# A transformer layer step on one core: small products moved to column quarters of TensorE, state products regrouped, and the loads and waits around them rearranged

## The chip, the cores and the metric

The kernel runs on one core of one Trainium2 chip, as one program. The metric is the device time of one execution in microseconds (us), inputs and outputs in device memory; smaller is better.

## What is computed

The reference is one step of a hybrid decoder layer for two groups of requests at once: a prompt of 256 tokens and 8 samples of 8 tokens each (past length 2048, paged cache). Model width is 1024, all in float32:

```python
x = x + 0.5 * swiglu_ffn(rmsnorm(x, ffn1_norm), ffn1_w_in, ffn1_w_out)      # 1024 -> 2 x 2816 -> 1024
h = rmsnorm(x, mix_norm)
z, xbc, dt_raw, q, kv, nsa_g, merge_g = jnp.split(h @ w_in_proj, cuts, axis=-1)
y_ssm, new_conv, new_ssm = mamba_mixer(...)        # conv, SSD with state (8, 32 heads, 64, 128) for the samples
q = rmsnorm(q.reshape(...), qk_norm[0]) * (HEAD_DIM ** -0.5)                # 16 heads of 64
o, new_win = nsa_fn(...)       # three branches: compressed blocks of 32 rows, top-16 blocks of 64, window of 512
mix = (gm[..., :D_MODEL] * (y_ssm @ w_branch_ssm) + gm[..., D_MODEL:] * (o @ w_branch_attn)) @ w_out
x = x + mix
x = x + 0.5 * swiglu_ffn(rmsnorm(x, ffn2_norm), ffn2_w_in, ffn2_w_out)
```

The compressed keys and values are `silu((rows + pe) @ w1) @ w2` over blocks of 32 rows, of the prompt and of the whole cache; relative biases come from a table of 32 buckets.

## The kernel before

All activations are kept transposed, features on the 128 partitions and the 320 tokens (256 of the prompt, 64 of the samples) along the free axis. A product with a big weight is a call of `dense` (L332). The weights come in 245 blocks of 128x1024 numbers, one after the other, through `w_load` (L300) on SyncE's DMA queue into buffers named `wraw`. ScalarE casts a block to its high part `wh` (`w_hi`, L314), VectorE subtracts that to get the low part `wl` (`w_lo`, L323); both are fp32r, the matmul form in which one pass suffices. TensorE then does three products for each of the 8 slices of 128 rows: high weight by high activation (L342), high by low (L343), low by high (L344), 24 products a block, each with 320 columns. Other products are in plain fp32 and appear in the trace as two instructions each.

The order of everything is set by the Python program. `dense` is its backbone: FFN1, then the projections (q and k, v, xBC, merge gates, z), the two branch products, the output product, FFN2. All other work is written as generators that `Sched.tick` steps between the slices of `dense`, by a credit that grows with `RATE`; `yield from wait(n)` lets n steps pass, and `S.defer(n, f)` calls f after 2n ticks, that is n quarters of a block. Each engine executes its own instructions strictly in the order so written, and the DMA queues of SyncE (SP) and GpSimd (POOL) do too.

The small work that the change touches, in order of time:

- During FFN1 the generator `cmp_stream` compresses the cache. It first turns the bias table into `trev` with products against a one-hot matrix `oh` (L638). `positions` (L599) sums 16 products of a slice of `w1` (128x128, stationary) with one column of position embedding (L602), once for keys and once for values. `cmp_keys` ends that work with two groups of four products (L733).
- `prompt_bias` (L840) loads the prompt's bias rows and a 128x128 `flip` matrix (L849) into `blob`, loads `tb` and `cb`, bias rows for the samples (`load_bias`, L832, 8 DMAs each), and multiplies by `flip` (L855).
- For each of the 12 blocks of q and k, the squares are summed over each head by one fp32 product with 24 output rows (L1870). `qk_norm` takes roots on 24 partitions and spreads them to the 128 feature rows by an fp32 product with a contraction over 24 rows (L873), again once per block.
- `prompt_cmp` compresses the prompt's rows: 16 fp32 products of a slice of `w1` with 32 columns (L1053), twice.
- `ssd` (chunks with the products L1637 and L1658, POOL multiplications L1627) and `sample_chunks` (state update of the samples) run during the xBC, merge and z projections. There are 32 states of 128x512 (`h`, 4 quarters q times 8 samples b), loaded by `load_h` (L1726) four ahead into 6 buffers, stored by `store` (L1679). Two at a time they are multiplied with `cz` on two column quarters of 32 (L1772); each is scaled on POOL (L1775), and a product `bz` x (`xh`, `xl`) is added: L1778 with 128 contraction rows, L1779 with 64, both fp32r with 512 columns; VectorE adds the result to `h` (L1780).
- `Squares` (L355) collects squares for a norm: `acc` on POOL or VectorE, then 12 instructions with one output column (L392: 3 token groups, `acc` and the last square apart).
- The sample attention loads pages `KV` (L1384) and multiplies them in eight tiles at once (L1431). `early_bias` (L1386) loads its bias rows, 16 DMAs on SP's queue (L1393).

Of the kernel before, what the change touches and what calls it, by code (L numbers as in the profile page):

```python
# [22 lines left out]
NB = 8  # L23
T = 8
# [19 lines left out]
_C = {}  # L44
_off = 0
for _n, _w in (("id", 128), ("sq", 47), ("sg", 7), ("tm", 8), ("gsum", 32), ("ex", 128), ("ss", 128), ("trp", 128),
               ("trs", 64), ("rm", 8), ("flip", 128), ("gs", 384), ("gp", 48)):
    _C[_n] = (_off, _w)
    _off += _w
# [8 lines left out]
def constants():  # L58
# [8 lines left out]
    a = np.zeros((128, 47)); a[p, 22 + p // 64] = 1; put("sq", a)  # L67
# [48 lines left out]
RATE = (0.59, 1.2, 0.9, 1.5, 0.85, 1.0, 1.0)  # L116
# [5 lines left out]
class Sched:  # L122
# [8 lines left out]
    def defer(self, n, f):  # L131
        self.later.append([n, f])
# [62 lines left out]
def step_kernel(ctx, tc, I, O):  # L195
# [102 lines left out]
    NRAW, SA = 2, 2  # L298
# [33 lines left out]
    def dense(unit, xh, xl, out, cut=1, extra=None):  # L332

        k0, K = 0, sum(n for _, n in unit)
        for i, n in unit:
# [3 lines left out]
            for k in range(n):  # L339
# [7 lines left out]
                if k == 1:  # L347
                    w_lo()
# [5 lines left out]
    class Squares:  # L354


        def __init__(self, n, delay=0):
            self.n, self.i, self.delay = n, 0, delay
# [28 lines left out]
        def sums(self):  # L387
            self.col = bank("pt", (128, 3))
            for i in range(3):
                n = 128 if i < 2 else 64  # L390
                for s in (self.acc, self.last):
                    pe.matmul(self.col[:n, i : i + 1], s[:, 128 * i : 128 * i + n], ones[:, 0:1], start=s is self.acc,  # L392
                              stop=s is self.last)
# [118 lines left out]
    for i in range(4):  # L512
        sp.dma_start(x[:, 2 * i : 2 * i + 2, :], I["xT"][:, 2 * i : 2 * i + 2, :])
        if i == 1:
            w_load()
# [5 lines left out]
    kraw = kT.rearrange("p b (a d) -> p b a d", a=2)  # L521
    kss = cp.tile([128, NB, 2], F32, name="kss")
    krs = cp.tile([128, NB, 2], F32, name="krs")
    pew = cp.tile([128, 2], F32, name="pew")
    rel = fp.tile([NBK + 1, 32], F32, name="rel")
# [72 lines left out]
    def positions(c):  # L598
        p = bank("po", (128, 1))  # L599
        for j in range(16):  # L600
            o = P_PE + 16 * c + j
            pe.matmul(p, w1raw(c)[:, j, :], par[:, o : o + 1], start=j == 0, stop=j == 15)  # L602
        v.tensor_copy(pew[:, c : c + 1], p)
        release(("w", c))

    def cmp_stream():
# [14 lines left out]
        yield  # L621
        g.memset(rel, -BIG)
# [3 lines left out]
        oht = fp.tile([NBK + 1, TL - 2048], F32, tag="hid", bufs=1, name="oht")  # L626
        sp.dma_start(oh, I["oh"][:, 0:2048])
        sp.dma_start(oht, I["oh"][:, 2048:])
# [6 lines left out]
        for k in (0, 320, 640, 960, 1280, 1600, 1920, 2048):  # L635
            n = min(NT, 2048 - k) if k < 2048 else TL - k
            p = bank("sc", (32, NT))
            pe.matmul(p[:, :n], rel, oh[:, k : k + n] if k < 2048 else oht, start=True, stop=True)  # L638
# [3 lines left out]
            yield  # L642
        release("oh")
        for q in range(4):
# [3 lines left out]
        positions(0)  # L648
        split_hi(0, 0)
        load(2)  # L650
        yield
        split_lo(0, 0)
# [3 lines left out]
        for s in range(NS):  # L656
            c, b = divmod(s, NB)
            ph = bank("sc", (128, 256))
            for q in range(4):
# [23 lines left out]
                if s == NB - 1:  # L683
                    split_w1(1, q)
                    if q == 3:
                        positions(1)
# [31 lines left out]
    def cmp_keys():  # L718
# [10 lines left out]
        yield from wait(4)  # L729
# [82 lines left out]
    cmpP = w1t[:, 4096:5120].rearrange("p (c a b i) -> p c a b i", c=2, a=2, b=2)  # L812
    q0 = ExitStack()
    pq = q0.enter_context(tc.tile_pool(name="pq", bufs=1))
    tb = pq.tile([128, 8], F32, name="tb")
# [1343 lines left out]
```

## Time and profile before

| what | value |
|---|---|
| median of 3 runs | 1389.86 us (1389.57 to 1399.72) |
| the profiled execution, its own time | 1398.44 us |
| its span in the trace | 1396.4 us |
| mean granted TensorE clock | 0.961 |
| busy: PE, DVE, ACT, POOL | 1329.4, 866.0, 592.8, 363.5 us |
| moved by DMA | 251.66 MB, 180 GB/s over the span |

A profile page shows one execution. "PE" is TensorE's matmuls, "PEld" its weight loads, DVE is VectorE, ACT ScalarE, POOL GpSimd, SP SyncE. A row such as `L342 PE MATMUL ps_pd<-hh,wh 128*128 128x320 f32 x1320 | 452.5, 343 | 4.5 ...` reads: line, engine, operation, output and inputs by the program's names, the tile of the array in use (contraction rows by output columns), the moving operand, how many, then busy time, mean ns of one, and the idle time just before them with what ended it. Matmuls overlap: the durations are longer than the distance from start to start, so what one costs is read from the starts in the timeline. PEclk is the share of the full clock that TensorE was granted.

### The profile page before, as it was taken

The page shows a single profiled execution, that of the slowest core. Times are in us where ns is not written, and L with a number is a line of the kernel's source. Part 1 is how long each engine was busy: PE and PEld are TensorE (multiplying, and loading weights), DVE is VectorE, ACT ScalarE, POOL GpSimd, SP SyncE. Part 2 cuts the span into 40 slices and gives each one's busy share as a digit, 9 for nine tenths or more (in the row PEclk, how much of TensorE's full clock was granted, in tenths as well). Part 3 has the DMA queues.
Part 4 walks back from the last instruction along what each step waited for, and adds up shares of the span by engine and source line. Part 5 has one row for each costly group of instructions (what it writes and reads, how often), then busy time and mean ns, then how long its engine had stood idle before and what let it go on. Part 6 is the DMA issues. An engine that isn't in the chain of part 4 may idle for free.

```text
span 1396.4 us, 28186 instructions
## 1 busy us (share of the span) xinstructions
PE 1329.4 (95%) x10583; PEld 1177.7 (84%) x10583; DVE 866.0 (62%) x1862; ACT 592.8 (42%) x1152; POOL 363.5 (26%) x616
## 2 busy tenths in 40 slices
PE   8999999999979999889989989799999999999998
PEld 7899999999858878677877756577677999999998
DVE  5577656655556457866567657657767766666533
ACT  4454543445434324446544343255555344333322
POOL 2222212222000216554444435233340010000000
PEclk9999999999989999889999999999999999999999
DMA  7556656666544325421177686778894443444453
GB/s 258 164 192 201 221 184 198 210 205 201 209 100 126 125 96 198 182 91 61 50 197 214 190 237 181 290 249 314 267 333 148 168 140 134 149 149 151 148 171 110
DMA packets 107041, 251.66 MB, mean 180 GB/s; under 512 B 23208, under 2 KB 49849, under 8 KB 104953
## 3 DMA queue, kind: packets, MB, share of 16 engines
q1 hardware_dynamic: 89946, 198.27, 44.2%
q0 software_dynamic: 16960, 51.61, 11.1%
q8 instruction: 83, 1.36, 0.4%
q14 instruction: 52, 0.43, 0.1%
HBM read 235.11 MB, written 23.10 MB: 185 GB/s over the span
## 4 chain that ended last, share of the span: by engine, by line
PE 72%; DVE 11%; DMA 5%; issue 4%; ACT 4%; SPq 2%; POOL 1%; POOLq 0%; ACTq 0%; DVEq 0%
PE ps_pd L342 18%; PE ps_pd L343 16%; PE ps_pd L344 16%; DVE wl L323 3%; PE ps_sc L671 2%; PE ps_sc L672 2%; PE ps_sc L681 2%; ACT wh L314 2%; PE ps_sc L1431 2%; DVE cvo L1198 2%; PE ps_po L1471 1%; DMA out_ssmS<-h 1%; PE ps_pt L1457 1%; PE ps_po L1319 1%; PE ps_sc L1270 1%
## 5 line engine op out<-in xcount | busy, mean ns | idle before, releaser
L323 DVE TENSOR_TENSOR wl<-wraw,wh 128x1024 fp32r<-128x1024 f32 (+1 forms) x245 | 302.0, 1233 | 266.9 <-ACT wh L314 266.4
L342 PE MATMUL ps_pd<-hh,wh 128*128 128x320 f32 x1320 | 452.5, 343 | 4.5 <-ACT hh L751 1.8
L343 PE MATMUL ps_pd<-hl,wh 128*128 128x320 f32 x1320 | 418.0, 317 | 1.6 <-DVE hl L450 1.4
L344 PE MATMUL ps_pd<-hh,wl 128*128 128x320 f32 x1320 | 417.2, 316 | 0.0
L314 ACT CAST wh<-wraw 128x1024 fp32r<-128x1024 f32 (+1 forms) x245 | 252.7, 1031 | 167.2 <-PE ps_pd L343 125.0
L342 PEld LDWEIGHTS ps_pd<-hh,wh 128*128 128x128 f32 x1320 | 257.4, 195 | 44.6 <-issue 32.8
L343 PEld LDWEIGHTS ps_pd<-hl,wh 128*128 128x128 f32 x1320 | 257.6, 195 | 10.2 <-issue 5.3
L344 PEld LDWEIGHTS ps_pd<-hh,wl 128*128 128x128 f32 x1320 | 256.5, 194 | 0.0
L342 PE MATMUL ps_pd<-ah,wh 128*128 128x320 f32 x352 | 109.4, 311 | 0.0
L344 PE MATMUL ps_pd<-ah,wl 128*128 128x320 f32 x352 | 108.7, 309 | 0.0
L343 PE MATMUL ps_pd<-al,wh 128*128 128x320 f32 x320 | 98.7, 309 | 0.0
L563 POOL DMA_DIRECT2D pg<-in_cache x136 | 74.3, 547 | 73.6 <-DVE pgl L575 30.6
L235 POOL TENSOR_SCALAR ah<-ff 128x320 fp32r<-128x320 f32 x44 | 20.1, 458 | 277.9 <-DVE ff L478 277.8
L575 DVE TENSOR_TENSOR pgl<-pg,pgh 128x512 fp32r<-128x512 f32 x128 | 82.4, 685 | 15.1 <-ACT pgh L568 14.9
L1384 POOL DMA_DIRECT2D KV<-in_cache x102 | 55.0, 539 | 104.3 <-PE ps_po L1471 68.5
L473 ACT ACTIVATE sg<-sg 128x320 f32<-128x320 f32 x44 | 20.8, 472 | 135.1 <-DVE sg L472 135.0
L568 ACT CAST pgh<-pg 128x512 fp32r<-128x512 f32 x128 | 72.6, 616 | 9.0 <-PE ps_sc L672 7.3
L671 PE MATMUL ps_sc<-pgh,w1h 128*128 128x256 f32 x256 | 68.6, 289 | 2.5 <-ACT pgh L568 2.5
L672 PE MATMUL ps_sc<-pgh,w1l 128*128 128x256 f32 x256 | 68.6, 288 | 0.0
L342 PEld LDWEIGHTS ps_pd<-ah,wh 128*128 128x128 f32 x352 | 66.1, 188 | 0.5
L344 PEld LDWEIGHTS ps_pd<-ah,wl 128*128 128x128 f32 x352 | 66.1, 188 | 0.0
L343 PEld LDWEIGHTS ps_pd<-al,wh 128*128 128x128 f32 x320 | 60.2, 188 | 0.0
(453 smaller groups left out, 2250.2 us busy)
## 6 DMA issues: line engine op xcount, KB each, us to landing
wraw<-in_wproj SPq DMA_DIRECT2D x77, 512.0 KB
KV<-in_cache POOLq DMA_DIRECT2D x102, 256.0 KB, 5.4
wraw<-in_w1in SPq DMA_DIRECT2D x44, 512.0 KB
wraw<-in_w2in SPq DMA_DIRECT2D x44, 512.0 KB
pg<-in_cache POOLq DMA_DIRECT2D x136, 128.0 KB, 4.1
pg<-in_cache SPq DMA_DIRECT2D x120, 128.0 KB
wraw<-in_w1out SPq DMA_DIRECT2D x16, 512.0 KB
h<-in_ssm SPq DMA_DIRECT2D x32, 256.0 KB
```

The costliest lines, as they stand in the source:

```text
L314: a.copy(h[:, :n], st["raw"][i][:, :n])
L323: v.tensor_tensor(l[:, :n], st["raw"].pop(i)[:, :n], st["hl"][i][0][:, :n], op=ALU.subtract)
L342: pe.matmul(out, wh[:, s], xh[:, kk, :], start=kk == 0, stop=False)
L343: pe.matmul(out, wh[:, s], xl[:, kk, :], start=False, stop=False)
L344: pe.matmul(out, wl[:, s], xh[:, kk, :], start=False, stop=kk == K - 1)
L563: e.dma_start(page(s, half)[:, i, :], I["cache"][ds(r, 1), :, 256 * c : 256 * c + 256].rearrange("o p f -> p (o f)"))
L568: a.copy(h[:, 8 * half : 8 * half + 8, :], page(s, half)[:, :, 64 * q : 64 * q + 64])
L575: v.tensor_tensor(l[:, 8 * half : 8 * half + 8, :], page(s, half)[:, :, 64 * q : 64 * q + 64], h[:, 8 * half : 8 * half + 8, :], op=ALU.su ...
L671: pe.matmul(ph, wh[:, j, :], h[:, :, j, :], start=q + j == 0, stop=False)
L672: pe.matmul(ph, wl[:, j, :], h[:, :, j, :], start=False, stop=False)
L681: pe.matmul(ph, wh[:, j, :], l[:, :, j, :], start=False, stop=q + j == 6)
L1384: e.dma_start(t[:, j, :], I["cache"][ds(r, 1), :, 512:1024].rearrange("o p f -> p (o f)"))
```

## The change

Line numbers with "after" are those of the changed kernel.

1. Column quarters: squares of four blocks of q and k at a time go to four quarters of 32 output columns (L1907 after, 3 groups). `positions` (L608 after) and the prompt's compression (L1083 after) swap their operands: a 32-column slice is stationary, `w1` moves, four quarters in turn, and a join product with `four32` (L615 and L1089 after) adds the quarters up.
2. Roots: taken on all 128 partitions, split into `qrh` and `qrl`, and spread with two fp32r products over 128 rows (L903 after) in place of one fp32 product over 24 rows.
3. `tb` and `cb` are no longer loaded from `trev`; 24 small products in FFN1 (L667 after, 8, 63 and 1 columns) compute them. `flip` is loaded during FFN1, `prompt_bias` is started ahead of the loads of `w1c`.
4. State update: four states at a time on four quarters (L1810 after), `xl` has 128 rows like `xh` (L1815 and L1816 after), `load_h` comes ahead of the store, five ahead into 8 buffers.
5. `Squares` may fold the last square into `acc` on VectorE, which leaves one product where there were two (z groups and the final norm).
6. Waits and rates: `cmp_keys` 4 to 7, six more steps before the first sample chunk, `WS` 8 to 4, `NRAW` 2 to 3, `w_lo` one slice later, `RATE[4]` 0.85 to 0.88, the descriptor space for software DMAs 8192 to 4096, `defer` keeps its list sorted.

The diff, cut to what the prediction speaks of:

```diff
-W0, W1, W2, W3, WS, EB = 3, 3, 6, 1, 8, 2
+W0, W1, W2, W3, WS, EB = 3, 3, 6, 1, 4, 2
...
-    NRAW, SA = 2, 2
+    NRAW, SA = 3, 2
...
-                if k == 1:
+                if k == 2:
                     w_lo()
...
         def gather(self, e):
-            if 1 < self.i < self.n:
+            if 1 < self.i < self.n + self.fold:
                 e.tensor_tensor(self.acc, self.acc, self.last, op=ALU.add)
 
         def add(self, x):
             self.square(x)
-            self.gather(g)
+            self.gather(v if self.i == self.n else g)
...
-                for s in (self.acc, self.last):
+                parts = [self.acc] if self.fold else [self.acc, self.last]
+                for s in parts:
...
     def positions(c):
-        p = bank("po", (128, 1))
+
+        p = bank("po", (128, 128))
         for j in range(16):
-            o = P_PE + 16 * c + j
-            pe.matmul(p, w1raw(c)[:, j, :], par[:, o : o + 1], start=j == 0, stop=j == 15)
-        v.tensor_copy(pew[:, c : c + 1], p)
+            o, r = P_PE + 16 * c + j, 32 * (j % 4)
+            pe.matmul(p[r : r + 32, :], par[:, o : o + 32], w1raw(c)[:, j, :], start=j < 4, stop=j >= 12)
+        pz = tp.tile([128, NT], F32, tag="sq", name="pz")[:, 0:128]
+        v.tensor_copy(pz, p)
         release(("w", c))
+
+        def join():
+            p = bank("po", (128, 1))
+            pe.matmul(p, pz, four32[:, 0:1], start=True, stop=True)
+            v.tensor_copy(pew[:, c : c + 1], p)
+
+        return join
...
+        p = bank("sc", (128, 72))
+        last = lambda t: oht[:, 6 - t : 7 - t] if t < 7 else oh[:, 2047:2048]
+        for o, n, src in ((0, 8, lambda t: oht[:, 7 - t : 15 - t]), (8, 63, lambda t: oh[:, 38 - t : 2048 - t : 32][:, 0:63]),
+                          (71, 1, last)):
+            for t in range(T):
+                pe.matmul(p[:, o : o + n], relz[:, 7 - t : 135 - t], src(t), start=t == 0, stop=t == T - 1)
+        a.copy(kcv[:, 2048:2120], p)
         release("oh")
+        sp.dma_start(flip, I["con"][:, C_KEEP : C_KEEP + 128])
...
-        yield from wait(4)
+        yield from wait(7)
...
-        flip = st["blob"][:, 4600:4728]
-        sp.dma_start(flip, I["con"][:, C_KEEP : C_KEEP + 128])
-        load_bias(tb, PAST, 8)
-        load_bias(cb, 31, 64, 32)
         yield from wait(8)
...
-            pe.matmul(bc, st["sel"][:, 128 * i : 128 * i + 128], rs, start=True, stop=True)
+            for x_ in range(2):
+                pe.matmul(bc, st["sel"][:, i, :], rhl[x_], start=x_ == 0, stop=x_ == 1)
...
+            part = bank("sc", (128, 128))
+            for j in range(16):
+                r = 32 * (j % 4)
+                pe.matmul(part[r : r + 32, :], cmpP[:, c, j].rearrange("p a b n -> p (a b n)"), w1b[:, c, j, :],
+                          start=j < 4, stop=j >= 12)
+            pz = st["blob"][:, 2688:2816]
+            v.tensor_copy(pz, part)
+            yield from wait(2)
             ph = bank("sc", (128, 32))
-            for j in range(16):
-                rhs = cmpP[:, c].rearrange("p a b (n j) -> p (a b) n j", j=16)[:, :, :, j]
-                pe.matmul(ph, w1b[:, c, j, :], rhs, start=j == 0, stop=j == 15)
+            pe.matmul(ph, pz, four32, start=True, stop=True)
...
-        NH, AHEAD = 6, 4
+        NH, AHEAD = 8, 5
...
-            xl = sx.tile([64, 512], F32R, tag="xl", bufs=1, name="xl")
+            xl = sx.tile([128, 512], F32R, tag="xl", bufs=1, name="xl")
...
                 weigh(q, 2)
                 yield
+                if q == 0:
+                    yield from wait(6)
                 stage_b(q, 2)
...
-                    if b % 2 == 0:
-                        for x_ in range(2):
-                            r = 32 * ((b + x_) % 4)
-                            pe.matmul(py[r : r + 32, :], cz[:, b + x_, :], pend["h", j + x_], start=b + x_ < 4,
-                                      stop=b + x_ >= 4)
+                    if b % 4 == 0:
+                        for x_ in range(4):
+                            r = 32 * x_
+                            pe.matmul(py[r : r + 32, :], cz[:, b + x_, :], pend["h", j + x_], start=b == 0, stop=b == 4)
...
-                    pe.matmul(p, bz[:64, b, :], xl, start=False, stop=True)
+                    pe.matmul(p, bz[:, b, :], xl, start=False, stop=True)
                     v.tensor_tensor(h0, h0, p, op=ALU.add)
+                    load_h(j + AHEAD)
                     store("outH")
                     pend["outH"] = O["ssmS"][b, :, 512 * q : 512 * q + 512], h0
-                    load_h(j + AHEAD)
...
+    def squares_of(k, four):
+        o = _C["sq"][0] + 22 - 2 * k
+        for x_, s in enumerate(four):
+            pe.matmul(ssq[32 * x_ : 32 * x_ + 32, :], con[:, o : o + 32], s, start=k == 0, stop=k == 2)
...
-        S.defer(3, lambda i=i, o=o, s=s: pe.matmul(ssq, con[:, o : o + 24], s, start=i == 0, stop=i == 11))
+        if i % 4 == 3:
+            S.defer(3, lambda k=i // 4, four=four: squares_of(k, four))
+            four = []
...
-            sq = Squares(4)
+            sq = Squares(4, fold=True)
...
-    sq = Squares(8, 3)
+    sq = Squares(8, 5, True)
```

How the rows stand on an engine is shown for three places. The first is TensorE in the state update: `ps_po<-h` is a state with `cz`, `ps_sc<-xh,bz` and `xl,bz` the added product, the others dense products. Before:

```order
L344 MATMUL ps_pd<-hh,wl 128x320
L1772 MATMUL ps_po<-h_8460,cz 32x512
L1772 MATMUL ps_po<-h_8468,cz 32x512
L1778 MATMUL ps_sc<-xh,bz 128x512
L1779 MATMUL ps_sc<-xl,bz 128x512
L1778 MATMUL ps_sc<-xh,bz 128x512
L1779 MATMUL ps_sc<-xl,bz 128x512
L342 MATMUL ps_pd<-hh,wh 128x320
```

and after:

```order
L347 MATMUL ps_pd<-hh,wl 128x320
L1810 MATMUL ps_po<-h_8228,cz 32x512
L1810 MATMUL ps_po<-h_8230,cz 32x512
L1810 MATMUL ps_po<-h_8232,cz 32x512
L1810 MATMUL ps_po<-h_8234,cz 32x512
L1815 MATMUL ps_sc<-xh,bz 128x512
L1816 MATMUL ps_sc<-xl,bz 128x512
L1815 MATMUL ps_sc<-xh,bz 128x512
L1816 MATMUL ps_sc<-xl,bz 128x512
L345 MATMUL ps_pd<-hh,wh 128x320
L346 MATMUL ps_pd<-hl,wh 128x320
L347 MATMUL ps_pd<-hh,wl 128x320
```

Four states stand together where two stood; the second half of their added products follows some dense rows later, without states ahead of it. The second place is SP's queue in the same stage. Before:

```order
L305 DMA wraw<-in_wproj 128x1024
L1679 DMA out_ssmS<-h_8557 128x512
L1726 DMA h_8872<-in_ssm 128x512
L1679 DMA out_ssmS<-h_8591 128x512
L1726 DMA h_8880<-in_ssm 128x512
```

and after:

```order
L308 DMA wraw<-in_wproj 128x1024
L1761 DMA h_9096<-in_ssm 128x512
L1714 DMA out_ssmS<-h_8722 128x512
L1761 DMA h_9104<-in_ssm 128x512
L1714 DMA out_ssmS<-h_8730 128x512
```

A load of the next state stands ahead of the store of an earlier one, where it stood behind it. The third place is SP's queue at the start of the projections. Before:

```order
L830 DMA w1t<-in_w1c 128x2048 x2
L1178 DMA scv<-in_sconv 128x576
L305 DMA wraw<-in_wproj 128x1024 x3
L847 DMA blob<-trev 64x4x256 x4
L849 DMA blob<-in_con 128x128
L837 DMA tb<-trev 16x8 x8
L837 DMA cb<-trev 16x64x1 x8
```

and after:

```order
L308 DMA wraw<-in_wproj 128x1024 x4
L810 DMA xsp<-x 128x2560
L875 DMA blob<-trev 64x4x256 x4
L1891 DMA w1t<-in_w1c 128x2048 x2
L308 DMA wraw<-in_wproj 128x1024 x6
```

The bias rows now stand ahead of `w1t` and of the weight loads, and the matrix `flip` and the 16 small loads are gone from here.

More of the change, by code (lines that the diff above doesn't have):

```diff
@@ L131, in defer @@
     def defer(self, n, f):
-        self.later.append([n, f])
+        i = len(self.later)
+        while i and self.later[i - 1][0] > n:
+            i -= 1
+        self.later.insert(i, [n, f])
     def flush(self):
@@ L521, in step_kernel @@
     kraw = kT.rearrange("p b (a d) -> p b a d", a=2)
+    tb, cb, flip = kcv[:, 2048:2056], kcv[:, 2056:2120], kcv[:, 2120:2248]
     kss = cp.tile([128, NB, 2], F32, name="kss")
@@ L524, in step_kernel @@
     pew = cp.tile([128, 2], F32, name="pew")
[L525 removed]
+    four32 = cp.tile([128, 32], F32, name="four32")
     held, LAG, numbers = [], 1, {}
@@ L647, in cmp_stream @@
             yield
-        positions(0)
+        for q in range(4):
+            gcopy(four32[32 * q : 32 * q + 32, :], ident[32 * q : 32 * q + 32, 32 * q : 32 * q + 32])
+        join = positions(0)
         split_hi(0, 0)
@@ L651, in cmp_stream @@
         yield
+        join()
         split_lo(0, 0)
@@ L685, in cmp_stream @@
                     if q == 3:
-                        positions(1)
+                        join = positions(1)
+                if (s, q) == (NB, 0):
+                    join()
                 if q == 3:
@@ L859, in selector @@
     def selector():
-        st["sel"] = st["blob"][:24, 2048:3584]
-        gcopy(st["sel"].rearrange("p (j d) -> p j d", d=64), ident[:24, :24].unsqueeze(2).to_broadcast([24, 24, 64]))
-        yield
-    def qk_norm(ssq):
-        rs = st["blob"][:24, 1664 : 1664 + NT]
-        tmp = [tp.tile([128, NT], F32, tag="sg", name="qrx")[:24] for _ in range(2)]
-        rsqrt(rs, ssq, 1.0 / 64, [24, NT], pa, "qr", tmp)
+        st["sel"] = pa.tile([128, 12, 128], F32R, name="sel")
+        id4 = ident.rearrange("p (x r) -> p x r", x=4)
+        for k in range(3):
+            gcopy(st["sel"][:, 4 * k : 4 * k + 4, :].rearrange("p x (h d) -> p x h d", h=2),
+                  id4[:, :, 2 * k : 2 * k + 2].unsqueeze(3).to_broadcast([128, 4, 2, 64]))
+            yield
+    def qk_norm(ssq):
+        rs = st["blob"][:, 1664 : 1664 + NT]
+        tmp = [tp.tile([128, NT], F32, tag="sg", name="qrx") for _ in range(2)]
+        rsqrt(rs, ssq, 1.0 / 64, [128, NT], pa, "qr", tmp)
+        rhl = [pa.tile([128, NT], F32R, name=f"qr{x_}") for x_ in "hl"]
+        split(*rhl, rs)
         gq = pa.tile([128, 1], F32, name="gq")
@@ L1849, in done @@
         yield IDLE
-    early = chain(cmp_keys(), prompt_bias(), selector(), until("gates"), both(gates_rows(), decays()))
+    bias_ = prompt_bias()
+    next(bias_)
+    for c in range(2):
+        sp.dma_start(w1b[:, c], I["w1c"][:, c])
+    early = chain(cmp_keys(), bias_, selector(), until("gates"), both(gates_rows(), decays()))
     S.rate = RATE[1]
```

53 lines of the change are left out of this document (28 added, 25 removed).

## Prediction

> **What bounds the kernel now.** I read the page first, then TensorE's timeline around each piece of small work, then the waits of TensorE, the chain, and windows with the granted clock.
>
> ```profile
> PE 1329.4 (95%) x10583; PEld 1177.7 (84%) x10583; DVE 866.0 (62%) x1862; ACT 592.8 (42%) x1152; POOL 363.5 (26%) x616
> PE   8999999999979999889989989799999999999998
> PEclk9999999999989999889999999999999999999999
> PE 72%; DVE 11%; DMA 5%; issue 4%; ACT 4%; SPq 2%; POOL 1%; POOLq 0%; ACTq 0%; DVEq 0%
> ```
>
> TensorE is busy in 95% of the span and makes 72% of the chain that ends last; no other engine is near. The low digits in PE and PEclk stand at the same slices: around the start of the projections, in the prompt's attention and in the state update. So the time is the sum of what TensorE does, of gaps, and of stretches at a lower clock, and each edit is costed in these three kinds.
>
> Since matmuls overlap, a product's cost is read from starts. One unit of the state update (two states) between dense products:
>
> ```profile
> 735.40 0.31 PE L344 MATMUL ps_pd<-hh,wl 128*128 128x320 f32 x1
> 735.64 1.05 PE L1772 MATMUL ps_po<-h,cz 128*32 128x512 f32 x4
> 736.62 0.50 PE L1778 MATMUL ps_sc<-xh,bz 128*128 128x512 f32 x1
> 737.05 0.49 PE L1779 MATMUL ps_sc<-xl,bz 64*128 64x512 f32 x1
> 737.47 0.50 PE L1778 MATMUL ps_sc<-xh,bz 128*128 128x512 f32 x1
> 737.90 0.50 PE L1779 MATMUL ps_sc<-xl,bz 64*128 64x512 f32 x1
> 738.33 0.41 PE L342 MATMUL ps_pd<-hh,wh 128*128 128x320 f32 x1
> 738.58 0.31 PE L343 MATMUL ps_pd<-hl,wh 128*128 128x320 f32 x1
> 738.73 0.31 PE L344 MATMUL ps_pd<-hh,wl 128*128 128x320 f32 x1
> 738.88 0.31 PE L342 MATMUL ps_pd<-hh,wh 128*128 128x320 f32 x1
> ```
>
> Dense products start 0.147 us apart (the last three rows), 0.46 ns a column. From L344 at 735.40 to L343 at 738.58 are 3.18 us, of which two dense steps are 0.29: the unit costs 2.89. Two things stand out. The four instructions of L1772 take 0.98 for two states. And L1778 and L1779 start 0.43 apart, where 512 columns at the dense rate would be 0.235. They alternate between 128 and 64 contraction rows. The dense product behind the last of them also shows 0.41 instead of 0.31, and the next one follows after 0.25 instead of 0.147, though its own form is unchanged. So I read the missing 0.2 as the price of changing the tile, about 0.1 before and 0.1 behind.
>
> The Trainium skill, "TensorEngine Tiling (Array Packing)", Key Properties, says that changing the tiling mode drains TensorE. These rows agree; by that rule every alternation that disappears is a gain, and every new small tile between dense products is a loss.
>
> **The change, part by part.** Negative is faster.
>
> *State update.* In the new order four states take one L1810 group, then 2 and 2 added products, all with 128 rows. Four quarters at once should cost what two do: in the attention eight tiles run in one such time,
>
> ```profile
> 919.75 1.02 PE ps_sc L1431 x16
> 915.91 1.11 PE ps_pt L392 x12
> ```
>
> sixteen instructions of 512 columns in 1.02 us (first row). So four states: 0.98, entry and exit 0.2 to 0.3, eight added products of 0.235, together 3.1 us, where two units are 5.78. Saved 2.7, eight times: -21.4. Bounds: if 0.43 is the price of 512 fp32r columns whatever the tile, four states cost 4.65 and the gain is 9; nothing makes it larger than about 23.
>
> *Squares of q and k, and roots.*
>
> ```profile
> 400.56 0.31 PE L344 MATMUL ps_pd<-hh,wl 128*128 128x320 f32 x1
> 400.80 0.72 PE L1870 MATMUL ps_po<-sq,con 128*24 128x320 f32 x2
> 401.70 0.30 PE L343 MATMUL ps_pd<-hl,wh 128*128 128x320 f32 x1
> ...
> 485.77 0.31 PE L344 MATMUL ps_pd<-hh,wl 128*128 128x320 f32 x1
> 486.01 0.80 PE L873 MATMUL ps_sc<-blob 24*128 24x320 f32 x2
> 487.00 0.31 PE L343 MATMUL ps_pd<-hl,wh 128*128 128x320 f32 x1
> ```
>
> By the same reckoning one L1870 costs 1.14 - 0.29 = 0.85 and one L873 1.23 - 0.29 = 0.94, tile changes included. Twelve of L1870 (10.2) become three groups at the price of one each (2.6): -7.6. Twelve of L873 (11.3) become 24 dense-like products of 0.147 (3.5) without a tile change: -7.7. Rooting 128 instead of 24 partitions costs the same time on ScalarE and VectorE, and the split is two more operations there, with DVE busy for 62%: nothing on the path, and 1 to 2 us if the spreading starts that much late.
>
> *Positions and the prompt's compression.*
>
> ```profile
> 487.58 0.31 PE L344 MATMUL ps_pd<-hh,wl 128*128 128x320 f32 x1
> 487.73 3.78 PE L1053 MATMUL ps_sc<-w1t 128*128 128x32 f32 x32
> 491.33 0.61 PE L342 MATMUL ps_pd<-hh,wh 128*128 128x320 f32 x1
> ```
>
> 32 instructions take 3.60 us, 0.112 each, though they have 32 columns only; it is a floor. L602 (one column, 32 instructions) is the same form, twice. In the new form 16 products of 128 columns run on four quarters, that is four rounds of two passes. A pass of 512 columns takes about 0.45 (half of L1772's 0.98), so one of 128 some 0.112: 0.9, plus a tile change 0.2 and the join 0.22, 1.3 in all. Saved 2.3 each, four times: -9.2. At worst the quarters do not overlap: 32 x 0.112 + 0.4, which is 0.4 slower each.
>
> *The new burst.* `tb` and `cb` are computed by 24 products of 8, 63 and 1 columns, 48 instructions at the floor of 0.112 and a tile change: +5.6. The trace of before has no such row; between one and two floors per product the bounds are 2.7 and 5.6, and plain fp32 shows two instructions everywhere, so 5.6. The 16 small loads removed in exchange were not waited for by TensorE as such.
>
> *Fold.* Twelve L392 take 1.11 (row above); six in five places: -2.8. Each adds one VectorE addition of about half a microsecond ahead of them, hidden by the blocks in between; without that cover +0.5 each.
>
> *Clock.* These windows (columns: stretch, length, PE busy, PEld, DVE, ACT, POOL, granted clock, DMA share, GB/s) hold the low stretches that the edits touch:
>
> ```profile
> 56.00:66.00 10.00, 10.00 (x55) 10.00 (x55) 4.40 (x8) 2.06 (x4) 3.52 (x7) 0.66 0.70 207
> 231.00:239.00 8.00, 8.00 (x39) 8.00 (x39) 3.73 (x7) 1.50 (x4) 4.02 (x8) 0.57 0.86 251
> 405.00:417.00 12.00, 7.56 (x27) 4.66 (x26) 1.88 (x2) 2.90 (x5) 0.00 (x0) 0.72 0.61 83
> 487.00:499.00 12.00, 12.00 (x61) 10.07 (x61) 3.34 (x6) 1.60 (x3) 0.00 (x0) 0.72 0.15 45
> 714.00:724.00 10.00, 6.51 (x39) 6.39 (x40) 4.88 (x11) 5.01 (x12) 5.33 (x3) 0.66 0.39 119
> 803.00:813.00 10.00, 5.96 (x15) 2.71 (x15) 4.00 (x6) 1.31 (x2) 1.81 (x3) 0.66 1.07 298
> ```
>
> Length times (1 - clock) is 3.4 us in each. Three of them (56, 231, 487) stand behind the bursts L602, L602 and L1053, with PE busy throughout: a stretch of 3.6 us of tiny products is followed by a lower clock. These bursts shrink to 1.3, so I count 3 x 3.4 as gone, and as the new burst is 5.6 long, one comes back: -6.8. Bounds 0 and -10.2.
>
> The Trainium skill, "TensorE: Matmul & The Clock Gate", section Why this matters for your kernels, ties the drop to idle gaps of over about 3 us. Here it comes without a gap, so by that rule alone neither the old bursts nor the new one would cost any clock, and the sum would be 6.8 higher; the trace decides.
>
> *Waits.*
>
> ```profile
> PE ps_pt L1637 <- POOL abs L1627: 5.4, 1, 5.4
> PE ps_pt L392 <- ACT sq L365: 5.1, 4, 1.8
> PE ps_sc L855 <- DMA blob<-in_con: 4.4, 1, 4.4
> PE ps_sc L1778 <- ACT btok L1608: 4.4, 1, 4.4
> PE ps_sc L733 <- DVE kcv L727: 2.5, 1, 2.5
> ...
> PE ps_po L1772 <- DMA h<-in_ssm: 0.3, 1, 0.3
> ...
> SPq L1726 <- DMA out_ssmS<-h: 43.0, 15, 6.1
> ```
>
> (What waited, for what: total, times, longest.) L855 waits for `flip`, which now comes in FFN1, with the bias rows ahead of `w1t` in SP's queue: up to 4.4 and the clock stretch at 405 (3.4), I take -6, since the bias rows themselves must still land. `cmp_keys` waits three steps more before L733, while dense products run: -1.5 of 2.5. The six steps before the first chunk give POOL's L1627 time: of 5.4 and 3.4 at 714, -6; late next is the whole state update, some 3 blocks behind where it was. At 803 L1778 waits for work whose root is SP: the load of a state stood behind a store and waited 43.0 us on stores in all, and weights and `ab` stood behind that. With 8 buffers and the load first, -4 of 4.4 and 3.4. The last L392 gets two more quarters of a block: -1. Together -18.5; bounds 0 (the next late thing takes each place) and -28.
>
> *New waits.* The state update ends later, so its stores and the attention's `KV` loads come together:
>
> ```profile
> PE ps_sc L1431 <- DVE ms L1444: 6.0, 1, 6.0
> 819.25 5.57 DMA h<-in_ssm
> 889.02 12.84 DMA KV<-in_cwin
> ```
>
> The chain already spends 12.84 us on one KV landing, and L1431 waits 6.0 there. `WS` lowered moves the attention closer: +4, bounds -2 and +9. And a group of four needs its fourth state when the group begins; that load is issued only two states ahead, and one took 5.57 to land: +3, bounds 0 and 45. The third `wraw` buffer, the later `w_lo`, the smaller descriptor space and the rate I put at 0, bounds -3 and +3: in three of the six windows above DMA is busy for less than half the time, and none of these edits adds a transfer.
>
> **Sum.** Products -21.4 - 7.6 - 7.7 - 9.2 - 2.8 + 5.6 = -43.1; clock -6.8; waits -18.5; new waits +7. Together -61.4. The profiled execution (1398.4) would go to 1337; it stood 8.6 above the median of the runs, 1389.9, from which the forecast is 1328.5, rounded to 1328.
>
> **Rivals.**
>
> - *Only the products.* Every wait that goes is replaced by the next late one, and the clock falls as often as before. For it: 18.5 us of the sum hang on waits that are partly for loads, and at 803 DMA is busy all the time, at 298 GB/s. Against it: three clock stretches follow bursts, not waits. Time 1389.9 - 43.1 = 1347.
> - *512 columns cost 0.43 in any tile.* For it: no fp32r product with 512 columns and 128 rows stands alone in the trace. Against it: the 0.41 of the dense product behind. Time 1328 + 12 = 1340.
> - *All of it.* Every wait and stretch listed goes and nothing new comes: -43.1 - 6.8 - 28 = -78, 1312.
> - *Slower: the fourth state.* TensorE waits in each of the eight groups for the load issued last. Each wait can reach the 6.1 for which SP waited before such a load and the 5.57 of its landing: 8 x 11.7 = 93, in place of the 3 counted, gives 1328 + 90 = 1418. It decides from (61.4 + 3) / 8 = 8 us a group on. For it: SP is one queue, and a load in it still needs a buffer that a store has emptied. Against it: the load now precedes the store, there are two buffers more, and L1772 waited for `h` just once, for 0.3 us, at four ahead.
> - *The quarters do not overlap*: squares and state products then cost as before, positions a little more, and 7.6 + 8 + 10.8 us of the gain are lost: 1354. The rows of L1431 speak against it.
>
> **How the numbers follow.** Forecast 0.52; only the products 0.23; 512 columns 0.07; all of it 0.11; quarters 0.03; the fourth state 0.04. What this kernel's measurement can tell from no change is about 1%, 1376 to 1404. The fourth state in full lies above that, at three quarters of its price inside: slower by more 0.02, within 1% 0.04 (half of it the upper tails of the other cases), faster by more 0.94. The range from 1300 to 1360 holds the first five but for their tails: the low end is "all of it" with 12 more, the high end "only the products" with 13 more for new waits.
>
> **What would show it.** Right: four L1810 and eight added products per four states, the latter about 0.235 apart; L1907 in three groups; L903 at 0.147; no low clock behind L608 and L1083, but one behind L667; no waits of over 2 us at `flip`, L733 and the first chunk. Wrong: added products still 0.43 apart, a wait of L1810 for `h`, a longer wait of L1431 for KV, or as many low stretches as before.

## The result, and the profile after

The changed kernel takes 1352.56 us (median of 4 runs, 1349.23 to 1360.85) against 1394.73 for the kernel before in the same session; the ratio is 0.9699, 95% interval 0.9658 to 0.974. That is 42 us faster where 61 were forecast. The profiled executions give the same difference: spans of 1396.4 and 1354.2, 42.2 us.

Rows of the page after that answer to those of before:

```profile
PE 1290.9 (95%) x10609; PEld 1164.3 (86%) x10609; DVE 877.8 (65%) x1872; ACT 593.0 (44%) x1154; POOL 372.1 (27%) x624
PE   7999999999999999889998898898999999999998
PEclk8799999999989998889999999799999998999999
```

TensorE is still busy in 95% of the span. The low digits at the start of the projections have become fewer, but the first two slices have become worse. The 7 in PEclk near the end of the state update is not a new low stretch: it is the landing of `KV`, which was there before and is cut otherwise by the slices (windows below). The granted clock was 0.961 before and 0.964 after, so low clock cost at most (1 - 0.961) x 1396.4 = 54.5 us and costs at most (1 - 0.964) x 1354.2 = 48.8.

The waits of TensorE after (what waited, for what: total, times, longest):

```profile
PE ps_po L1810 <- DMA h<-in_ssm: 9.1, 5, 3.6
PE ps_po L1506 <- ACT R L1512: 5.2, 3, 3.5
PE ps_po L1354 <- ACT qn L1358: 3.6, 1, 3.6
PE ps_sc L655 <- DMA pg<-in_oh: 3.2, 1, 3.2
PE ps_sc L1466 <- DMA KV<-in_cache: 3.1, 2, 2.8
...
PE ps_pt L1672 <- POOL abs L1662: 1.0, 2, 0.6
```

The waits named in the forecast are gone: `flip` and L733 do not appear any more, POOL's `abs` went from 5.4 to 1.0. In front stands now a wait that was 0.3: the state products for `h`.

Both programs have the same 5784 dense products, so the start of every 192nd of them (eight blocks) is a common ruler. Worked out from these starts, the change gained or lost by stage (us, minus is faster):

| blocks | what runs there besides dense products | difference |
|---|---|---|
| 0 to 8 | first norm, bias table, the new burst | +17.7 |
| 8 to 64 | positions, cache compression | -11.0 |
| 64 to 88 | norm, bias, squares, roots, prompt's compression | -27.0 |
| 88 to 112 | convolution, prompt's attention | -1.6 |
| 112 to 144 | state update, start of the sample attention | -23.5 |
| 144 to end | sample attention, branch products, FFN2 | +3.2 |

One of these differences flatters the change. The profile of before spent 309.7 us in blocks 8 to 64. Three other profiles of the same code there (the single edits in the kernel before, below) spent 304.4 to 304.8, with 3.4 us of half clock behind each position sum where this one has 6.8, and with none at 204. About 5 of the 11.0 belong to this one profile.

The products did what the forecast said. One group of the state update, first half and a dense product around it:

```profile
713.09 0.31 PE L347 MATMUL ps_pd<-hh,wl 128*128 128x320 f32 x1
713.33 1.06 PE L1810 MATMUL ps_po<-h,cz 128*32 128x512 f32 x8
714.32 0.50 PE L1815 MATMUL ps_sc<-xh,bz 128*128 128x512 f32 x1
714.66 0.40 PE L1816 MATMUL ps_sc<-xl,bz 128*128 128x512 f32 x1
714.89 0.39 PE L1815 MATMUL ps_sc<-xh,bz 128*128 128x512 f32 x1
715.13 0.39 PE L1816 MATMUL ps_sc<-xl,bz 128*128 128x512 f32 x1
715.36 0.31 PE L345 MATMUL ps_pd<-hh,wh 128*128 128x320 f32 x1
715.50 0.31 PE L346 MATMUL ps_pd<-hl,wh 128*128 128x320 f32 x1
```

Eight instructions, four states, take 0.99, as two states did. L1815 and L1816 follow each other after 0.23 where it was 0.43, and the dense product behind them shows 0.31 and is followed after 0.14: no tile change is left there. The first L1815, right behind the 32-column tile, still pays one (0.34 to the next). The rival of 512 columns is refuted by these rows.

That is the first group of four of a quarter q, with all its states there. The second group of the same quarter:

```profile
722.46 0.31 PE L347 MATMUL ps_pd<-hh,wl 128*128 128x320 f32 x1
722.70 1.06 PE L1810 MATMUL ps_po<-h,cz 128*32 128x512 f32 x6
725.38 1.05 PE L1810 MATMUL ps_po<-h,cz 128*32 128x512 f32 x2 [1.63 <-DMA h<-in_ssm]
726.36 0.50 PE L1815 MATMUL ps_sc<-xh,bz 128*128 128x512 f32 x1
```

Three states run, TensorE waits 1.63 us for the fourth, and that one then takes 0.98 alone, as long as four together. So a late fourth state costs its wait and a pass of its own.

The squares, the roots and the prompt's compression, likewise:

```profile
419.15 0.31 PE L347 MATMUL ps_pd<-hh,wl 128*128 128x320 f32 x1
419.39 0.46 PE L1907 MATMUL ps_po<-sq,con 128*32 128x320 f32 x2
...
420.32 0.31 PE L346 MATMUL ps_pd<-hl,wh 128*128 128x320 f32 x1
...
481.24 0.31 PE L347 MATMUL ps_pd<-hh,wl 128*128 128x320 f32 x1
481.48 1.08 PE L1083 MATMUL ps_sc<-w1t 128*32 128x128 f32 x32
482.49 0.41 PE L345 MATMUL ps_pd<-hh,wh 128*128 128x320 f32 x1
482.74 0.31 PE L346 MATMUL ps_pd<-hl,wh 128*128 128x320 f32 x1
...
483.33 0.31 PE L347 MATMUL ps_pd<-hh,wl 128*128 128x320 f32 x1
483.48 0.31 PE L903 MATMUL ps_sc<-qrh,sel 128*128 128x320 f32 x1
483.63 0.31 PE L903 MATMUL ps_sc<-qrl,sel 128*128 128x320 f32 x1
483.77 0.31 PE L345 MATMUL ps_pd<-hh,wh 128*128 128x320 f32 x1
```

By the prediction's reckoning a group of four squares costs 1.17 - 0.29 = 0.88, one spread of roots 0.29, the compression 1.50 - 0.29 = 1.21 and its join 0.22.

Much of the missing 19 us lies in the first blocks and in late states, with low clock beside them. Windows of after (stretch, length, busy times, granted clock, DMA share, GB/s):

```profile
30.00:47.00 17.00, 13.84 (x43) 9.14 (x42) 5.08 (x8) 4.11 (x7) 2.51 (x5) 0.60 0.46 153
56.00:70.00 14.00, 13.70 (x73) 13.42 (x72) 2.17 (x5) 3.24 (x7) 1.89 (x4) 0.63 0.22 71
...
853.00:873.00 20.00, 15.56 (x77) 8.41 (x77) 8.76 (x26) 6.33 (x15) 4.57 (x9) 0.66 0.89 326
```

The first lost 17 x 0.40 = 6.8 us, the second, with the burst L667, 5.2, the third, where `KV` lands, 6.8. The landing of `KV` in the kernel before lost 16 x 0.32 = 5.1:

```profile
896.00:912.00 16.00, 10.03 (x49) 6.48 (x47) 7.77 (x19) 7.03 (x15) 2.69 (x5) 0.68 0.82 329
```

### The profile page after: what moved, and what is told of

It is laid out like the page before. It is cut to its first block, busy times and chain, and to the rows that moved or that the text cites. A ratio compares the mean times of both kernels' runs of the same rounds, so it can differ in the third digit from the quotient of the medians.

```text
span 1354.2 us, 28228 instructions
## 1 busy us (share of the span) xinstructions
PE 1290.9 (95%) x10609; PEld 1164.3 (86%) x10609; DVE 877.8 (65%) x1872; ACT 593.0 (44%) x1154; POOL 372.1 (27%) x624
## 5 line engine op out<-in xcount | busy, mean ns | idle before, releaser
L326 DVE TENSOR_TENSOR wl<-wraw,wh 128x1024 fp32r<-128x1024 f32 (+1 forms) x245 | 305.4, 1248 | 178.2 <-ACT wh L317 175.5
L568 POOL DMA_DIRECT2D pg<-in_cache x136 | 74.2, 546 | 77.4 <-DVE pgl L580 30.8
```

Of the source, the lines that this page charges most:

```text
L326: v.tensor_tensor(l[:, :n], st["raw"].pop(i)[:, :n], st["hl"][i][0][:, :n], op=ALU.subtract)
L568: e.dma_start(page(s, half)[:, i, :], I["cache"][ds(r, 1), :, 256 * c : 256 * c + 256].rearrange("o p f -> p (o f)"))
```

## The experiments

Times are compared with the kernel before, run beside each; its median moves by a few us between sessions, so the ratio is what counts. Single edits of 3 to 10 us lie near the width of the intervals; for them the trace of the profiled execution is read with the same ruler of dense products. An insertion is the small work that stands between two dense products; it costs the distance of their starts less one dense step. The 16 units of the kernel before are such insertions too, with the slowed dense step behind them counted in.

**States loaded earlier.** In the changed kernel the load of a group's last state is issued one step ahead.

```diff
-        NH, AHEAD = 8, 5
+        NH, AHEAD = 10, 7
```

> The changed kernel with the states loaded seven ahead into ten buffers instead of five into eight. Theory: in the changed kernel the second group of four of each quarter waits for its fourth state (2.2 to 4.2 us at L1810), because that load is issued only one step earlier. With seven ahead it is issued a whole group earlier: the waits of L1810 for h (9.1 us in all) go below 2 us, the eight group insertions and eight second halves fall from 47.9 us to 30 to 36, and the time falls by 10 to 16 us against the changed kernel (about 1337 to 1342). Rival: DMA is saturated in this stage (about 300 GB/s), so earlier issue lands no earlier, and the time stays within 4 us of 1352.

Measured: 1347.38 us, ratio 0.9665 (0.9629 to 0.9701). That is 5 us where 10 to 16 were expected, and the interval overlaps that of the changed kernel. In the trace L1810 now waits once for `h` instead of five times and 9.1 us:

```profile
PE ps_po L1810 <- DMA h<-in_ssm: 3.8, 1, 3.8
```

All insertions of the state update sum to 40.4 us, 47.9 in the changed kernel. From block 112 to 144 the trace is 4.9 us shorter. So the late states are real, and loading them earlier gives 5 to 7.5 us; the theory had put all of the loss, and more, on the distance of the load.

One wait stayed, and SP's queue in that trace shows why:

```profile
743.62 10.73 SPq L1428 DMA_DIRECT2D bias<-trev  x16
754.40 0.58 SPq L1430 DMA_DIRECT2D wb<-in_wm  x1
755.09 0.61 SPq L1616 DMA_DIRECT2D abs<-ascr  x1
755.79 0.57 SPq L1616 DMA_DIRECT2D ab<-ascr  x1
756.46 0.54 SPq L308 DMA_DIRECT2D wraw<-in_wproj  x1
757.04 0.42 SPq L1761 DMA_DIRECT2D h<-in_ssm  x1
```

Sixteen small loads of the attention's bias take 10.7 us to issue, and the state's load stands behind them.

**Bias loads in four parts**, one for each step of the prompt's chunks:

```diff
+                if t % 4 == 3:
+                    yield
...
                 if i == EB:
                     yield from until("conv")
-                    early_bias()
+                    eb = early_bias()
+                if i >= EB:
+                    next(eb, None)
```

> The changed kernel with the 16 bias loads on SP's queue in the state update split in four groups of four, one per step of the prompt's chunks, instead of 16 at once (10.7 us of issuing at 743). Theory: the worst wait of L1810 (3.6 and 0.7 us at 758 to 767, with a low clock behind) is for states whose load stood behind these 16; it falls below 2 us and the time falls by 4 to 7 us. Rival: the transfers are late by bandwidth; no change within 3 us.

Measured: 1351.49 us, ratio 0.9693 (0.9649 to 0.9737): in the time no difference can be seen. In the trace:

```profile
PE ps_po L1814 <- DMA h<-in_ssm: 6.4, 5, 1.8
```

The longest wait fell from 3.6 to 1.8 (L1814 is here what L1810 was), and blocks 112 to 144 are 2.0 us shorter: 3.8 in the stretch with the bias loads, less 1.7 lost just ahead of it. The mechanism holds in the trace; the size was too high, and the time does not show it.

**Two states at a time in the changed kernel.**

```diff
-                    if b % 4 == 0:
-                        for x_ in range(4):
+                    if b % 2 == 0:
+                        for x_ in range(2):
```

> The changed kernel with two states at a time instead of four (L1810 in pairs). Theory of the fourth state: pairs find their states, so 10 to 13 us of waits go, while eight more groups of 0.98 and their tile changes cost about 9: within 4 us of the changed kernel. Rival, transfers set the pace: the waits stay and the pairs cost 8 to 10 us more (about 1361).

Measured: 1357.59 us, ratio 0.9725 (0.9691 to 0.976). The wait for `h` is no longer among the larger ones, and the 16 insertions sum to 42.7, 5.2 less than with four; what came before and after them took it back, and from block 112 to 144 the trace is 1.3 us longer. The difference in the profile's span is 6.8, of which 2.4 lie in the first blocks where the code is the same. This does not decide between the two; it was asked again below, without the late loads.

**Without the burst.** The 24 products of L667 are taken out, the 16 small loads are back, behind those of `w1c`.

```diff
-        for o, n, src in ((0, 8, ...), (8, 63, ...), (71, 1, last)):
-            for t in range(T):
-                pe.matmul(p[:, o : o + n], relz[:, 7 - t : 135 - t], src(t), start=t == 0, stop=t == T - 1)
...
+    load_bias(tb, PAST, 8)
+    load_bias(cb, 31, 64, 32)
```

> The changed kernel without the 24 small products of L667; the bias rows for the samples are loaded by 16 small DMAs as before, but behind the loads of w1c. Theory: the burst costs 5.6 us of its own and 3 to 5 us of low clock, so the time falls by 8 to 11 us (about 1343). Rival: the 16 DMAs in SP's queue hold up the weight loads at the start of the projections and give 4 to 8 us back, so the gain is under 4 us.

Measured: 1347.74 us, ratio 0.9664 (0.9633 to 0.9695). By the ratios that is 5 us, between the theory (8 to 11) and the rival (under 4), and the interval overlaps that of the changed kernel. In the trace the first eight blocks are 11.0 us shorter, and the span 9.6. The start of the projections lost 1.2, no more. So in the trace the burst costs 10 to 11 us, its own 5.6 and 5.2 of clock. There it was not worth the loads that it replaced; how much of this the time keeps is not settled.

**w1 behind the one-hot matrix.**

```diff
-        load_w1(0)
         yield
...
         sp.dma_start(con[:, 128:], I["con"][:, 128:C_KEEP])
+        load_w1(0)
```

> The changed kernel with the 1 MB load of w1 moved behind the loads of the one-hot matrix in FFN1. Theory: the wait of L655 for that matrix (3.2 us) put the clock down for 13.65 us (6.8 us lost), so both go: 8 to 10 us faster (about 1343). Rival: the low clock comes from the sparse small products there and not from the wait: 2 to 3 us faster only, the low stretch at 32 us stays.

Measured: 1349.94 us, ratio 0.967 (0.9642 to 0.9698). The first eight blocks are 7.1 us shorter; L655 does not wait, and the low stretch of 13.65 us at 32 is gone, so it was the wait that put the clock down, and not the sparse products, which still run. The other traces agree: all six of the changed kernel in which `w1` is loaded first have a wait of 1.7 to 5.4 us there and 13.65 to 20.5 us of low clock behind it, and all four with the matrix first wait at most 0.5 us and have no such stretch. But the span of this execution is no shorter: blocks 120 to 144 were 5.7 us longer and other small pieces took the rest, with more low clock in the same code. The gain is seen at its place; the time alone does not show it.

**Two weight buffers and the first loads of before.**

```diff
-    NRAW, SA = 3, 2
+    NRAW, SA = 2, 2
...
-        if i % 2:
+        if i == 1:
```

> The changed kernel with two wraw buffers and the first loads in the order of before. Theory: the third weight block in flight stood ahead of the one-hot matrix in the DMA engines and made L655 wait 3.2 us; without it L655 waits under 1.2 us, the 13.65 us low stretch at 32 goes, and the first eight blocks take 6 to 10 us less; behind them within 3 us of the changed kernel. Rival: the third buffer is needed in the state update, where TensorE then waits for weights: 5 us or more are lost there.

Measured: 1356.42 us, ratio 0.9726 (0.9696 to 0.9755). Refuted: the first eight blocks were 1.2 us longer, with a low stretch of 17 us. TensorE now waited 3.5 us for a dense block's input there instead of for the matrix. The third buffer is not what made the start slow, and the kernel is no faster without it. Which of the edits brought the wait in is open: the kernel before also loads `w1` first, and its profile has no such wait.

**The full tile alone, in the kernel before.**

```diff
-            xl = sx.tile([64, 512], F32R, tag="xl", bufs=1, name="xl")
+            xl = sx.tile([128, 512], F32R, tag="xl", bufs=1, name="xl")
...
-                    pe.matmul(p, bz[:64, b, :], xl, start=False, stop=True)
+                    pe.matmul(p, bz[:, b, :], xl, start=False, stop=True)
```

> The kernel of before with one edit alone: xl has 128 rows, so that the added products of the state update all use the full tile. Theory of the tile change: 32 pairs of products at 0.43 each fall to 0.235, 64 x 0.2 = 12.8 us at most, so 10 to 13 us faster than before (ratio 0.991 to 0.993), with the distance from L1778 to L1779 at 0.23. Rival, 512 columns cost 0.43 in any tile: no change. Second rival, the stage is set by loads and stores of the states: the distance falls but waits grow by as much, under 4 us faster.

Measured: 1391.56 us, ratio 0.9972 (0.9948 to 0.9996), 4 us. A unit that waits for nothing falls from 2.89 to 2.10, which over 16 units is 12.6 us; the sum of the units falls from 58.1 to 53.3 only. The second rival comes nearest: 8 of the 12.6 went into waits.

This trace tells something else. Up to the state update its program is that of before, and still its first eight blocks took 61.0 us instead of 53.7. In its timeline:

```profile
25.73 1.03 PE L406 MATMUL ps_pt<-con,nrs 128*128 128x128 f32 x6
30.08 0.64 PE L342 MATMUL ps_pd<-hh,wh 128*128 128x320 f32 x1 [3.33 <-DVE sg L472]
```

and in one window of it, then the same window of the kernel before:

```profile
26.00:47.00 21.00, 17.67 (x58) 12.50 (x56) 7.33 (x11) 6.97 (x11) 2.50 (x5) 0.59 0.57 174
```

```profile
26.00:47.00 21.00, 19.08 (x106) 14.12 (x106) 10.02 (x15) 10.06 (x17) 4.25 (x9) 1.00 0.63 200
```

One wait of 3.3 us, and the clock stays low for 17 us though TensorE is busy for 17.67 of 21. The old code comes out with it in one profile of four and without it in three. In the changed kernel it is the rule: about 7 of the 17.7 us that its first eight blocks lost are of this kind, and only the order of the first loads took them away.

**The queue alone, in the kernel before**: load ahead of store, five ahead, eight buffers.

```diff
-        NH, AHEAD = 6, 4
+        NH, AHEAD = 8, 5
...
+                    load_h(j + AHEAD)
                     store("outH")
                     pend["outH"] = O["ssmS"][b, :, 512 * q : 512 * q + 512], h0
-                    load_h(j + AHEAD)
```

> The kernel of before with the order of the state loads alone changed: load ahead of the store, five ahead, eight buffers. Theory that SP's queue sets the pace of the state update: the 16 units (58.1 us, of which 46 are products) fall to 48 to 52 us and the time falls by 4 to 9 us (ratio 0.994 to 0.997). Rival, bandwidth: within 3 us of before.

Measured: 1385.86 us, ratio 0.9954 (0.9934 to 0.9973). The units sum to 53.0 where they were 58.1. The time agrees with the theory, and the units fell 1 us short of it.

**Both, in the kernel before.**

```diff
-        NH, AHEAD = 6, 4
+        NH, AHEAD = 8, 5
...
-            xl = sx.tile([64, 512], F32R, tag="xl", bufs=1, name="xl")
+            xl = sx.tile([128, 512], F32R, tag="xl", bufs=1, name="xl")
...
-                    pe.matmul(p, bz[:64, b, :], xl, start=False, stop=True)
+                    pe.matmul(p, bz[:, b, :], xl, start=False, stop=True)
                     v.tensor_tensor(h0, h0, p, op=ALU.add)
+                    load_h(j + AHEAD)
                     store("outH")
...
-                    load_h(j + AHEAD)
```

> The kernel of before with both: xl of 128 rows and the state loads ahead of the stores. xl alone took the 16 units from 58.1 to 53.3 us where its products lost 12.6. Theory that the rest was lost to late states: with both the units fall to 38 to 43 us, 15 to 20 us below before, more than the two alone together. Rival, other waits (chunks, POOL, KV) take it: not below 48 us, under 9 us in the time.

Measured: 1374.79 us, ratio 0.9882 (0.9852 to 0.9913). The units sum to 41.7. Alone the full tile gave 0.3% and the queue 0.5%; together they give 1.2%, 16 us. In the units the two alone took off 4.8 and 5.1, together 16.4, clearly more than the sum; in the times the intervals are too wide to say so.

**Four edits together on the changed kernel**: no burst, w1 behind the one-hot matrix, seven ahead in ten buffers, bias loads in four parts.

The burst is taken out as above; of the rest:

```diff
-        load_w1(0)
...
+        load_w1(0)
         yield from wait(2)
...
+                if t % 4 == 3:
+                    yield
...
+                if i >= EB:
+                    next(eb, None)
...
-        NH, AHEAD = 8, 5
+        NH, AHEAD = 10, 7
...
+    load_bias(tb, PAST, 8)
+    load_bias(cb, 31, 64, 32)
```

> The changed kernel with four edits together: no burst L667 (small loads behind w1c instead), w1 loaded behind the one-hot matrix, states seven ahead in ten buffers, the bias loads spread. Theory: the gains add, 9.6 + 7 + 4.5 + 4 = 25 us, about 1328. Rival: the state update and the KV loads behind it are bound by transfers that start at a given time, and what is gained ahead of them is lost there: 10 us, about 1342.

Measured: 1323.32 us, ratio 0.9505 (0.9477 to 0.9534), the lowest 1321.84 and the highest 1327.06. Its waits and its first blocks:

```profile
PE ps_po L1499 <- ACT R L1505: 5.2, 3, 3.5
PE ps_sc L1459 <- DMA KV<-in_cache: 4.0, 2, 3.5
PE ps_po L1345 <- ACT qn L1349: 3.6, 1, 3.6
```

```profile
26.00:47.00 21.00, 19.96 (x112) 14.74 (x111) 9.88 (x16) 9.44 (x16) 4.98 (x10) 1.00 0.66 223
```

The gains add where they were read, in the traces: 19.6 us in the first eight blocks (11.0 and 7.1 alone) and 12.3 from block 112 to 144 (4.9 and 2.0 alone), 34.0 in the spans. In the times the four give 27 us by the ratios, 29 by the medians; alone they gave 4.9, 4.0, 4.7 and 0.8, 14 in all. Whether the single times show too little or the edits help each other is not separated. `h` is not waited for any more, the insertions of the state update sum to 35.0, and the early low stretch is gone. The runs also lie within 5 us of each other, where those of the changed kernel spread over 12.

**That version with two states at a time.**

```diff
-                    if b % 4 == 0:
-                        for x_ in range(4):
+                    if b % 2 == 0:
+                        for x_ in range(2):
```

> The fastest version (no burst, w1 behind the one-hot matrix, states seven ahead in ten buffers, bias loads spread) with two states at a time in place of four. Theory: with the states in time a group costs 0.98 plus its tile change 0.2 and nothing waits, so pairs cost 8 x 1.2 = 9 us more (about 1332). Rival, fours still wait for their last state: 4 us more or less than the fours.

Measured: 1334.58 us, ratio 0.959 (0.957 to 0.9609), 11 us more where 9 were expected; the two intervals do not touch. With the states in time, four at once is worth having. The insertions sum to 41.0 against 35.0, so they show 6 of it; the rest stands between them and in low clock, of which there are 17.1 us at the `KV` landing against 13.65.

**That version with the sample attention later.**

```diff
-W0, W1, W2, W3, WS, EB = 3, 3, 6, 1, 4, 2
+W0, W1, W2, W3, WS, EB = 3, 3, 6, 1, 10, 2
```

> The fastest version with WS 10 in place of 4: the attention's first scores six steps later. Theory: the wait of L1466's counterpart for KV (3.5 us) and the 13.65 us low stretch behind it (6.8 us) go, as dense products fill the time: 5 to 10 us faster. Rival: the attention ends that much later and TensorE waits behind the branch product instead: no gain, or up to 5 us slower.

Measured: 1330.67 us, ratio 0.9548 (0.9519 to 0.9578). That is 6 to 7 us slower than without the edit, with intervals that just overlap. From block 128 to 144 the trace gained 14.6 us, with half of the low stretch there gone; from 144 to 160 it lost 21.3: the attention's products that moved there, and 8.5 us lost to low clock where there had been none. The rival holds: what was gained at the `KV` landing is paid later.

The six further steps before the first sample chunk, the rate, the later `w_lo` and the earlier `flip` were not tried alone.

## Why the prediction was right in sign and 19 us too far

*Products, -43.1.* Right. Twelve squares and twelve spreads were 10.1 and 11.1 and became 2.6 and 3.5 (-7.5 and -7.6 for -7.6 and -7.7). Four states cost 2.11 + 0.93 = 3.04 where nothing waits (3.1 forecast). A compression or position sum costs 1.21 and a join of 0.22 or more (1.3 forecast). The reading of 0.43 as 0.23 and a tile change of 0.2 was right in the changed kernel and again alone.

*The burst, +5.6 and 3.4 of clock.* Right in kind, 2 us small: its removal gave 11.0 in its place, in the trace.

*Clock, -6.8, and the clock within the waits.* Right at the three bursts, as the stretches behind the positions and the compression are gone. They were priced on one profile: three others of the same code lost 1.7 us behind each position sum, not 3.4. Wrong at `flip`: its wait went, but around the end of FFN1 10.2 us of half clock stand at 384 to 398 where 10.2 stood at 396 to 416 (0 to 10.2 in the other profiles of the changed kernel). And a new low stretch stands at the start (6.8 us), which was not in the forecast. Over the whole span low clock fell by 5.7.

*Waits, -18.5.* `flip`, L733 and the first chunk went as said. So did "-4 of 4.4 and 3.4" for SP's queue: the wait of 4.4 at L1778 has no counterpart after. The last L392 was put at -1; the fold and the delay together took 4.1 us of waits at L392.

*New waits, +7: the term that failed.* It is "+3, bounds 0 and 45" for the fourth state. Products of 46.2 in units of 58.1 left 11.8 us of waits and low clock before; after, 24.3 of products stand in 47.9 us of insertions, which leaves 23.6. Of these 16.7 are in the second groups of the four quarters, which cost 2.7, 8.5, 2.8 and 2.7 us more than a group that waits for nothing; the other 6.9 are less than the 11.8 by about what was forecast for SP's queue. So the term is 16.7 where 3 were counted, in four groups and not in eight. In three of them the fourth state is late, by 1.6 us, and then runs alone for 0.98, which the forecast had not priced. In the one of 8.5 the second state already waits 3.6 us: its load stands behind the 16 bias loads. I had argued that two more buffers and the new order suffice; the load for the last of four is still issued only two states ahead, and behind what else stands in SP's queue.

The other term, +4 for `KV`, did not come: waits of 6.0 before, 3.1 and 1.6 after, with 1.7 us more of low clock. That it and L392 erred the other way is luck, and hid part of the late states.

*Edits put at 0.* The reason given was a misreading: in two of the six windows DMA is busy for less than half the time (0.15 and 0.39), not in three. What the third buffer is worth was asked above; the others were not tried alone.

By stages, with each term put where its work runs, blocks 0 to 8 were forecast at +9.0 and came to +17.7, blocks 64 to 88 at -30.8 and came to -27.0, and those from 112 on at -28.2 and came to -20.3; the rest agrees within 2. So the 19 us are about 9 at the start, 4 around the end of FFN1 and 8 behind block 112, less 1 elsewhere. The four edits that went to the first and the third place recovered 27.

## What to carry to other kernels

When a change shortens the engine's work in a stage that also streams data, move the loads forward by as much in the same change; alone, the shorter products here kept 5 of 12.6 us in their stage, and with the loads moved the stage lost 16.4. Cost a grouping by the time at which its last input is issued, look at everything that stands ahead of it in that queue, and count the pass that a late member runs alone. A wait of 3.2 us in front of sparse work cost 6.8 us of clock more, so order the first loads by who needs them first.

## What the runs showed of the hardware

- A change of tile between neighbouring products costs about 0.2 us: 512 columns in alternating tiles of 128 and 64 rows 0.43 each, in one tile 0.23, in two kernels.
- Bursts of tiny products are often followed by half clock though TensorE hardly waits. Of the 16 bursts of 3.6 us with 1 or 32 columns in the four profiles that hold them, 12 were followed by 3.4 to 10.2 us of it; of the 40 that replace them, with 128 columns in 1.1 us, one was. The burst of 48 products with 8, 63 and 1 columns had 6.8 or 10.2 us in all six profiles that hold it. The Trainium skill, "TensorE: Matmul & The Clock Gate", Why this matters for your kernels, ties a drop in mid-kernel to idle gaps between bursts; the trace shows it without one.
- After a wait of 1.7 to 5.4 us the clock stayed low for 13.65 to 20.5 us, in seven profiles, while TensorE was mostly busy with dense products and sparse ones between them. Without the wait the same products ran at full clock (window from 26 to 47, 0.59 and 1.00). At half clock dense products start 0.27 us apart, 0.147 at full clock.
- Four products of 512 columns on four column quarters take 0.99 us together, and one that comes late takes 0.98 alone.
